# A two-layer hybrid backbone: 512-column projections, block transposes queued in the next block, other layouts and another order at the two ends

## The chip, the cores and the metric

The kernel runs on one core of a Trainium2 chip. The core has TensorE (PE: matrix products of 128x128 blocks of 32-bit numbers into PSUM, which has eight banks of 128x512), VectorE (DVE), ScalarE (ACT), GpSimd (POOL) and SyncE (SP), which here issues the loads from device memory. The metric is the device time of one launch in microseconds (us). Each kernel's runs are given by their median.

## The reference

```python
# layer 0: two recurrences as head groups, then a dense SwiGLU
u = modulate(rmsnorm(h), shift, scale)          # shift, scale: silu(cond) @ w_mod + b_mod
p = split(u @ w_in)                             # q, two gates, v, z of HGRN2; x, gate of RG-LRU
hg = gated linear attention over chunks of 64, both directions
rg = linear scan with gates of x, both directions
h = h + gate * (concat(rmsnorm(hg) * silu(z), rg * gelu(g)) @ w_out)
h = h + gate * ((silu(u2 @ w1) * (u2 @ w3)) @ w2)
# layer 1: neighbourhood attention, then top 2 of 8 experts
q, k, v = split(u @ w_qkv); q, k = rmsnorm per head
h = h + gate * (softmax(q k^T + bias, local window and all context keys) v @ w_o)
y = sum over the 2 best of 8 experts of weight_e * (silu(u2 @ w1[e]) * (u2 @ w3[e])) @ w2[e]
return h + gate * y                             # of the 256 latent tokens
```

There are 256 latent and 256 context tokens of width 1024; context tokens are modulated by a vector of their own. The hidden width is 2816, for the dense layer and for each expert. In the last layer only the latent tokens go through the experts.

## The kernel before

All weights are streamed from device memory once and the activations stay on the core. The loads go through one queue of SP, in program order, each into one of 15 slots of 1 MB; when no slot is free, the queue waits. Tokens are kept transposed (features on partitions, 512 tokens on columns).

A product of layer 0 and of the attention's projections is made in three matmuls (`mm3`, L157 to L160): each 32-bit operand is split into a high and a low part (`halves`, L131, on ACT and DVE: whi, wlo of the weights; Uhi, Ulo of the tokens), and high x high, high x low and low x high are summed. `proj_T` (L385) puts features on partitions, `proj_N` (L399) puts tokens there, in blocks of 256 columns: for each of two blocks and each tile of 128 tokens, 8 k-steps of three matmuls.

The beginning (L341 to L383): the two streams' tokens H0 are loaded, then blocks 2 and 0 of the modulation weights w_mod (scale and shift), the first chunks of w_in, and w_mod's blocks 3 and 1. `squares` (L306) and `rstd_rows` (L282) form the norm; `early_products` (L353) makes a row of modulation per block (L185), and `mod_finish` (L190) transposes it (L196). `modulate` (L321) writes Uhi and Ulo, first of k-steps 0 to 3, for which 48 matmuls follow, then of 4 to 7. In the recurrence that follows, steps of HGRN and matmuls of the projections share TensorE; the order is that of a scheduler with priorities, which writes it out ahead of time.

The experts (L1149 on): an expert has three blocks of hidden features (512, 512 and 384), a "unit" (e, j). `w13` makes silu(x w1) * (x w3) of up to 64 tokens of each of two tiles, on four 32-column strips of the array, and of a third group of 32 rows only if the expert has more than 64 tokens in a tile's share (`third_group`; experts 0, 1 and 3 take it here). `turn` (L1176) transposes a block's hidden rows hN into hT by matmuls with the identity, on 32-column strips; it is called in the next unit's w13 behind half of its k-steps. `down` (L1195) multiplies by w2, and `keep` (L1223) puts the expert's result into Y (three tiles of 128 rows hold four experts: 64 rows each in tiles 0 and 1, 32 each in tile 2). `gather` (L1097) collects the next experts' tokens with one-hot matrices (L1111, and L1064 for expert 0). After experts 3 and 7 `places` (L1239, one-hot matrices with the gates as values) and `scatter` (L1260) add Y back to the tokens; for experts 4 to 7 this stands around the last down() and at the end. `chores` is a list of such small works, of which one step is taken at each new weight chunk.

## Time and profile before

| | |
|---|---|
| runs (us) | 1697.43, 1701.37, 1702.54 |
| median | 1701.37 |
| profiled execution | 1702.45, its span 1700.7 |
| TensorE busy | 1598.6 of the span (94%) |
| VectorE, ScalarE, GpSimd busy | 721.1, 455.5, 56.0 |
| loads | 412.42 MB, mean 243 GB/s |

The profile is one execution. "Span" is the time from the first to the last instruction on record. Busy times of the engines overlap. A row such as `PE ... L1188 MATMUL ps_x<-ident,hN 128*32 128x128 f32 x64` is a run of 64 matmuls of line 1188 whose result lies in ps_x, made of ident and hN, on a 128x32 strip of the array; matmuls of 32-bit numbers on strips stand twice in the record. In brackets stands how long the engine was idle before, and what it waited for.

### The profile page before, as it was taken

The page shows a single profiled execution, that of the slowest core. Times are in us where ns is not written, and L with a number is a line of the kernel's source. Part 1 is how long each engine was busy: PE and PEld are TensorE (multiplying, and loading weights), DVE is VectorE, ACT ScalarE, POOL GpSimd, SP SyncE. Part 2 cuts the span into 40 slices and gives each one's busy share as a digit, 9 for nine tenths or more (in the row PEclk, how much of TensorE's full clock was granted, in tenths as well). Part 3 has the DMA queues.
Part 4 walks back from the last instruction along what each step waited for, and adds up shares of the span by engine and source line. Part 5 has one row for each costly group of instructions (what it writes and reads, how often), then busy time and mean ns, then how long its engine had stood idle before and what let it go on. Part 6 is the DMA issues. An engine that isn't in the chain of part 4 may idle for free. (4 is left out here: it accounts for less than half of the span.)

```text
span 1700.7 us, 29356 instructions
## 1 busy us (share of the span) xinstructions
PE 1598.6 (94%) x12668; PEld 1000.4 (59%) x12668; DVE 721.1 (42%) x1417; ACT 455.5 (27%) x795; POOL 56.0 (3%) x58
## 2 busy tenths in 40 slices
PE   6997989999999999999999999999999999998887
PEld 3675867788778788889984654343344334432222
DVE  6677456596874433678737520020202021201122
ACT  4574333433222222244536410010101010100000
POOL 0013141000000000000000000000000000000000
PEclk9999999999999999999998979999999999999999
DMA  9515123844475232534332298979999989999995
GB/s 342 170 63 173 50 75 124 295 140 149 149 246 174 87 99 99 173 115 159 125 124 76 103 364 302 352 275 398 414 415 413 416 352 411 414 414 412 410 400 229
DMA packets 153060, 412.42 MB, mean 243 GB/s; under 512 B 9552, under 2 KB 69328, under 8 KB 134864
## 3 DMA queue, kind: packets, MB, share of 16 engines
q1 hardware_dynamic: 152912, 410.28, 64.1%
q8 instruction: 113, 1.85, 0.5%
q14 instruction: 35, 0.29, 0.0%
HBM read 409.20 MB, written 1.05 MB: 241 GB/s over the span
## 5 line engine op out<-in xcount | busy, mean ns | idle before, releaser
L158 PE MATMUL ps_mm<-Uhi,whi 128*128 128x512 f32 (+1 forms) x576 | 223.5, 393 | 5.5 <-ACT Uhi L327 2.9
L1157 PE MATMUL ps_mm<-raw,X 128*32 128x512 f32 (+1 forms) x1920 | 212.1, 570 | 15.3 <-DMA raw<-in_moe_u 14.1
L160 PE MATMUL ps_mm<-Uhi,wlo 128*128 128x512 f32 (+1 forms) x576 | 222.4, 388 | 0.0
L159 PE MATMUL ps_mm<-Ulo,whi 128*128 128x512 f32 (+1 forms) x576 | 221.7, 388 | 0.0
L137 DVE TENSOR_TENSOR wlo<-raw,whi 128x1024 fp32r<-128x1024 f32 x134 | 164.9, 1239 | 114.7 <-ACT whi L137 109.9
L137 ACT CAST whi<-raw 128x1024 fp32r<-128x1024 f32 x134 | 139.1, 1049 | 274.0 <-PE ps_mm L159 208.9
L1157 PEld LDWEIGHTS ps_mm<-raw,X 128*32 128x32 f32 x1920 | 68.4, 111 | 140.8 <-issue 105.3
L1172 DVE TENSOR_TENSOR hN<-hs,ps_mm 128x512 f32<-128x512 f32 (+1 forms) x24 | 15.4, 643 | 300.4 <-PE ps_mm L1157 300.2
L158 PEld LDWEIGHTS ps_mm<-Uhi,whi 128*128 128x128 f32 x576 | 109.1, 191 | 31.6 <-ACT Uhi L327 3.3
L160 PEld LDWEIGHTS ps_mm<-Uhi,wlo 128*128 128x128 f32 x576 | 109.3, 190 | 23.6 <-issue 1.2
L159 PEld LDWEIGHTS ps_mm<-Ulo,whi 128*128 128x128 f32 x576 | 109.3, 190 | 23.5 <-issue 1.7
L1209 PE MATMUL ps_py<-raw,hT 128*32 128x512 f32 x928 | 113.4, 596 | 3.4 <-PEq L1142 1.7
L1170 ACT ACTIVATE hs<-ps_mm 128x512 f32<-128x512 f32 (+1 forms) x24 | 13.5, 561 | 374.2 <-PE ps_mm L1157 374.2
L408 PE MATMUL ps_mm<-whi,Uhi 128*128 128x256 f32 x384 | 110.9, 289 | 1.4 <-ACT Vn L547 1.0
L409 PE MATMUL ps_mm<-wlo,Uhi 128*128 128x256 f32 x384 | 109.7, 286 | 0.0
L410 PE MATMUL ps_mm<-whi,Ulo 128*128 128x256 f32 x384 | 109.6, 287 | 0.0
L236 DVE SCALAR_TENSOR_TENSOR macc<-raw,cond,macc 128x512 f32<-128x512 f32 x112 | 80.5, 748 | 6.4 <-DMA raw<-in_w_mod 5.7
L158 PE MATMUL ps_mm<-hh,whi 128*128 128x512 f32 (+1 forms) x224 | 77.9, 351 | 2.0 <-DVE H L688 1.6
L1157 PE MATMUL ps_mm<-wlo,X 128*32 128x512 f32 (+1 forms) x576 | 75.8, 555 | 3.8 <-DMA wlo<-in_moe_u 2.5
L160 PE MATMUL ps_mm<-hh,wlo 128*128 128x512 f32 (+1 forms) x224 | 77.7, 348 | 0.0
L159 PE MATMUL ps_mm<-hl,whi 128*128 128x512 f32 (+1 forms) x224 | 77.6, 347 | 0.0
L408 PEld LDWEIGHTS ps_mm<-whi,Uhi 128*128 128x128 f32 x384 | 72.8, 190 | 6.2 <-ACT Vn L547 2.4
(299 smaller groups left out, 2325.2 us busy)
## 6 DMA issues: line engine op xcount, KB each, us to landing
raw<-in_moe_u SPq DMA_DIRECT2D x83, 1024.0 KB, 13.1
raw<-in_moe_d SPq DMA_DIRECT2D x58, 1024.0 KB, 14.3
raw<-in_w_mod SPq DMA_DIRECT2D x48, 1024.0 KB, 5.4
raw<-in_ffn_w SPq DMA_DIRECT2D x33, 1024.0 KB, 5.3
raw<-in_moe_u SPq DMA_DIRECT2D x37, 768.0 KB, 10.8
wlo<-in_moe_u SPq DMA_DIRECT2D x45, 512.0 KB, 10.7
whi<-in_moe_u SPq DMA_DIRECT2D x45, 512.0 KB, 11.4
whi<-in_moe_d SPq DMA_DIRECT2D x30, 512.0 KB, 11.5
```

Source lines behind the costliest of these rows:

```text
L137: latest[:] = act.copy(hi, v), dve.tensor_tensor(lo, v, hi.bitcast(F32), op=OP.subtract)
L158: pe.matmul(o, sh, mh, start=start, stop=False)
L159: pe.matmul(o, sh, ml, start=False, stop=False)
L160: pe.matmul(o, sl, mh, start=False, stop=stop)
L236: dve.scalar_tensor_tensor(acc[s], w[:, j, :], c, acc[s], op0=OP.mult, op1=OP.add)
L408: pe.matmul(p, Uhi[:, k, tt], hi, start=k == 0, stop=False)
L409: pe.matmul(p, Uhi[:, k, tt], lo, start=False, stop=False)
L410: pe.matmul(p, Ulo[:, k, tt], hi, start=False, stop=k == KT - 1)
L1157: pe.matmul(p[b][32 * q:32 * q + 32, :], X[e][:, k, 32 * g:32 * g + 32], w[2 * b + a], start=k == 0, stop=k == KT - 1, tile_position=(0, 3 ...
L1170: act.activation(s[0][:, :fn], p[0], AF.Silu)
L1172: dve.tensor_tensor(h[0][:, :fn], s[0][:, :fn], p[1], op=OP.mult)
L1209: pe.matmul(PY[e][0][32 * q:32 * q + 32, :], hT_[:, c, CAP * a + 32 * g:CAP * a + 32 * g + 32], w[a][:, 512 * col:512 * col + 512], start= ...
```

## The change

Six edits.

1. The tokens (hT) and the modulation weights are laid out in device memory in the order in which they are read, so that each partition reads 8 KB in one piece (before: 1 KB of hT, 2 KB of w_mod).
2. Another order at the beginning: squares are made two k-slices at a time; the first chunk of w_in has 512 rows x 512 columns instead of 1024 x 256, and the second is loaded behind w_mod's blocks 3 and 1; the matmuls of three tiles for k-steps 0 to 3 come first, then the products of blocks 3 and 1, then the fourth tile's.
3. `proj_N` makes 512 columns at a time, with two chunks of 512 rows; all its tiles hold a PSUM bank until the second chunk. The norm of q and k (`qk_part`, `turn_qk`) follows in blocks of 512.
4. The first gather works on 32-column strips, and the second waits behind the first matmul of expert 0.
5. `turn` is made of 128x128 transposes, six for a full block, and is queued behind the fourth k-step of the next block. The third group's hidden rows lie in two halves on 128 partitions.
6. Y's rows are placed so that the last of four experts lies in tile 2 alone. Tiles 0 and 1 of experts 4 to 6 are scattered during expert 7, as chores; only tile 2 is left for the end. `keep` handles the third rows first.

```diff
+        if not kt:
+            v = raw.rearrange("p (k c) -> p k c", k=4)
+            sp.dma_start(v, src)
+            return v
...
-        return [stream(A["w_mod"][layer, 512 * half:512 * half + 512, 512 * blk:512 * blk + 512], 4, 512)
-                for half in range(2)]
-    def mod_products(p, ww):
-        for half, w in enumerate(ww):
+        return [stream(A["w_mod"][layer, blk, half]) for half in range(2)]
...
-    def squares(tp, h, s, acc):
+    def squares(tp, h, s, acc=None):
         c = slice(256 * s, 256 * s + 256)
-        for k in range(KT):
+        a = tp.tile([128, 2, NL], F32, name="sqa", tag="sqa", bufs=1)
+        for k in range(0, KT, 2):
             if k == 0:
-                act.activation(acc, h[:, k, c], AF.Square)
+                act.activation(a, h[:, k:k + 2, c], AF.Square)
             else:
-                sq = tp.tile([128, NL], F32, name="sq", tag="sq", bufs=2)
-                act.activation(sq, h[:, k, c], AF.Square)
-                dve.tensor_tensor(acc, acc, sq, op=OP.add)
+                sq = tp.tile([128, 2, NL], F32, name="sq", tag="sq", bufs=3)
+                act.activation(sq, h[:, k:k + 2, c], AF.Square)
+                dve.tensor_tensor(a, a, sq, op=OP.add)
+        acc = a[:, 0] if acc is None else acc
+        dve.tensor_tensor(acc, a[:, 0], a[:, 1], op=OP.add)
+        return acc
...
-            sp.dma_start(H0[:, :, NL * s:NL * s + NL], hT[:, :, NL * s:NL * s + NL])
+            sp.dma_start(H0[s], A["hT"][s])
...
+        def first_products(kk, tiles):
+            if not parts[kk]:
+                parts[kk] = [halves(wfirst[kk][:, 2 * i:2 * i + 2, :]) for i in range(2)]
+            for i in tiles:
+                for k in range(4):
+                    hi, lo = (x[:, k % 2, 128 * i:128 * i + 128] for x in parts[kk][k // 2])
+                    u = 4 * kk + k
+                    m = mm3(first[i], hi, lo, Uhi[:, u, :], Ulo[:, u, :], u == 0, u == KT - 1)
+            return m
...
-                wfirst = [stream(w_in[:, 2560 + 256 * m:2816 + 256 * m], KT, 256) for m in range(2)]
-            early_products(kk)
+                wfirst = [stream(w_in[0:512, 2560:3072], 4, 512)]
...
                 early.update((blk, mod_load(0, blk)) for blk in (3, 1))
-                first = [halves(v[:, :, 128 * i:128 * i + 128]) for v in wfirst for i in range(2)]
-                first = [(ps("mm"), hi, lo) for hi, lo in first]
-            for p, hi, lo in first if kk == 0 else ():
-                for k in range(4):
-                    mm3(p, hi[:, k, :], lo[:, k, :], Uhi[:, k, :], Ulo[:, k, :], k == 0, False)
+                wfirst.append(stream(w_in[512:1024, 2560:3072], 4, 512))
+                first = [ps("mm") for _ in range(4)]
+                m = first_products(0, range(3))
+                with behind(m):
+                    early_products(3)
+                with behind(m):
+                    m = early_products(1)
+                with behind(m):
+                    first_products(0, [3])
...
-    def proj_N(w, col, tiles, use, n=2):
-        for half in range(n):
-            w2 = weights(w[:, col + 256 * half:col + 256 * half + 256], KT, 256, "k")
+    def proj_N(w, col, tiles, use):
+        pp = {}
+        for kk in range(2):
+            w2 = weights(w[512 * kk:512 * kk + 512, col:col + 512], 4, 512, "k")
             for t in tiles:
-                p = ps("mm", 256)
+                p = pp[t] = ps("mm") if kk == 0 else pp[t]
                 tt = slice(128 * t, 128 * t + 128)
-                for k in range(KT):
-                    hi, lo = (x[:, k % 4, :] for x in w2[k // 4])
-                    pe.matmul(p, Uhi[:, k, tt], hi, start=k == 0, stop=False)
-                    pe.matmul(p, Uhi[:, k, tt], lo, start=False, stop=False)
-                    pe.matmul(p, Ulo[:, k, tt], hi, start=False, stop=k == KT - 1)
-                use(t, half, p)
+                for k in range(4):
+                    hi, lo = (x[:, k % 2, :] for x in w2[k // 2])
+                    u = 4 * kk + k
+                    pe.matmul(p, Uhi[:, u, tt], hi, start=u == 0, stop=False)
+                    pe.matmul(p, Uhi[:, u, tt], lo, start=False, stop=False)
+                    pe.matmul(p, Ulo[:, u, tt], hi, start=False, stop=u == KT - 1)
+                if kk:
+                    use(t, p)
             step()
...
-                pe.matmul(first[k // 4][:, CAP * (k % 4):CAP * (k % 4) + CAP], UN[:, t, 128 * k:128 * k + 128],
-                          DO[0][:, t, 0, :], start=t == 0 and k % 4 == 0, stop=t == 1 and k % 4 == 3)
+                for q in range(0, 128, 32):
+                    pe.matmul(first[k // 4][q:q + 32, CAP * (k % 4):CAP * (k % 4) + CAP],
+                              UN[:, t, 128 * k + q:128 * k + q + 32], DO[0][:, t, 0, :],
+                              start=t == 0 and k % 4 == 0, stop=t == 1 and k % 4 == 3, tile_position=(0, q))
...
+        after = opening if e2 == 0 else []
...
+                        with behind(*after):
...
-                at_half()
+                with behind(m):
+                    at_half()
...
-        dve.tensor_tensor(h[1][0:64, :fn], s[1][64:128, :fn], p[2][64:128, :], op=OP.mult)
+        for r, a, b in ((0, 0, 256), (64, 256, fn)):
+            dve.tensor_tensor(h[1][r:r + 64, 0:b - a], s[1][64:128, a:b], p[2][64:128, a:b], op=OP.mult)
...
-        for c0 in range(0, nc_, 2):
-            n = min(2, nc_ - c0)
-            p = ps("x", 2 * CAP * n)
-            for i, (r, w) in enumerate(((128, 64), (64, 32))):
-                for c in range(n):
-                    for q in range(0, 128, 32):
-                        f = 128 * (c0 + c) + q
-                        pe.matmul(sub(p[q:q + 32, :], 2 * CAP * c + 64 * i, [(CAP, 2), (1, w)]), h[i][0:r, f:f + 32],
-                                  ident[0:r, 0:r], start=True, stop=True, tile_position=(0, q), skip_group_check=True)
-            (act.copy if c0 else dve.tensor_copy)(hT_[:, c0:c0 + n, :].rearrange("p c t -> p (c t)"), p)
+        pp = [ps("x", 2 * CAP * n) for n in (2, nc_ - 2)]
+        for c, p in enumerate(pp):
+            for i in range(c, nc_, 2):
+                pe.transpose(sub(p, CAP * (i - c), [(CAP, 2), (1, 64)]), h[0][:, 128 * i:128 * i + 128], ident)
+        for c, p in enumerate(pp):
+            n = len(range(c, nc_, 2))
+            pe.transpose(sub(p, 64, [(2 * CAP, n), (CAP, 2), (1, 32)]), h[1][0:64 * n, 128 * c:128 * c + 128],
+                         ident[0:64 * n, 0:64 * n])
+        for c, p in enumerate(pp):
+            n = len(range(c, nc_, 2))
+            (act.copy if c else dve.tensor_copy)(sub(hT_[:, 0, :], 2 * CAP * c, [(4 * CAP, n), (1, 2 * CAP)]),
+                                                 p.rearrange("p (c t) -> p c t", c=n))
...
+        (k, at), (k3, at3) = PLACES[i]
+        for col in range(2):
             act.copy(t[64 * col:64 * col + 32, :], p[1][64 * col + 32:64 * col + 64, :])
         for col, c in enumerate(cols):
             r = slice(64 * col, 64 * col + 32)
             dve.tensor_tensor(t[r, :], t[r, :], p[1][r, :], op=OP.add)
-            dve.tensor_tensor(Y[32 * i:32 * i + 32, 2, c], t[r, :], gt2r[r, c], op=OP.mult)
+            dve.tensor_tensor(Y[at3:at3 + 32, k3, c], t[r, :], gt2r[r, c], op=OP.mult)
+        for col, c in enumerate(cols):
+            r = slice(64 * col, 64 * col + 64)
+            dve.tensor_tensor(Y[at:at + 64, k, c], p[0][r, :], gt2r[r, c], op=OP.mult)
...
+    PLACES = [((0, 0), (1, 64)), ((0, 64), (1, 96)), ((1, 0), (2, 96)), ((2, 0), (2, 64))]
+    DTS = {}
...
-    def half():
-        for DT in places(0):
+    def half(h, tiles):
+        for DTS[h] in places(h):
             yield
         for t, g in SETS:
             p = ps("x")
-            for i in range(3):
-                scatter(p, DT, t, g, [i])
+            for i in range(tiles):
+                scatter(p, DTS[h], t, g, i, i == 0, i == tiles - 1)
                 yield
             scattered(p, t, g)
...
-            for DT in places(1):
-                pass
-            acc = [ps("mm") if i < 3 else ps("x") for i in range(4)]
-            for p, (t, g) in zip(acc, SETS):
-                scatter(p, DT, t, g, [0])
         down(e, j)
         if (e, j) == (3, len(EBLOCKS) - 1):
-            chores.append(half())
-    for i in (1, 2):
-        for p, (t, g) in zip(acc, SETS):
-            scatter(p, DT, t, g, [i])
+            chores.append(half(0, 3))
+        if (e, j) == (6, len(EBLOCKS) - 1):
+            chores.append(half(1, 2))
+    while chores:
+        chore()
+    acc = [ps("mm") if i < 3 else ps("x") for i in range(4)]
+    for p, (t, g) in zip(acc, SETS):
+        scatter(p, DTS[1], t, g, 2, True, True)
...
-        "hT": np.concatenate([I["ctx"][0], I["x"][0]], axis=0).T,
-        "w_mod": I["w_mod"], "b_mod": I["b_mod"], "w_in": I["ev_w_in"][0], "w_out": I["ev_w_out"][0],
+        "hT": np.stack([I["ctx"][0], I["x"][0]]).reshape(2, NL, KT, 128).transpose(0, 3, 2, 1),
...
+        "w_mod": np.asarray(I["w_mod"]).reshape(2, 2, 4, 128, 12, 512).transpose(0, 4, 1, 3, 2, 5), "b_mod": I["b_mod"], "w_in": I["ev_w_in"][0], "w_out": I["ev_w_out"][0],
```

What the order shows on TensorE at three places follows (line, operation, result<-operands, shape, count). First the beginning: before, from the end of the first k-steps' matmuls (L158 to L160) over the products of the modulation (L185) and its transposes (L196) to the next matmuls.

```order
L160 MATMUL ps_mm<-Uhi,wlo 128x512
L158 MATMUL ps_mm<-Uhi,whi 128x512
L159 MATMUL ps_mm<-Ulo,whi 128x512
L160 MATMUL ps_mm<-Uhi,wlo 128x512
L185 MATMUL ps_md<-raw,cond 32x512 x16
L196 MATMUL ps_x<-ident,modrow 128x128 x8
L158 MATMUL ps_mm<-Uhi,whi 128x512 x3
```

Of the change, the same place; L162 to L164 are the three matmuls, L188 the products, L200 the transposes.

```order
L162 MATMUL ps_mm<-Uhi,whi 128x512
L163 MATMUL ps_mm<-Ulo,whi 128x512
L164 MATMUL ps_mm<-Uhi,wlo 128x512
L188 MATMUL ps_md<-raw,cond 32x512 x16
L200 MATMUL ps_x<-ident,modrow 128x128 x4
...
L200 MATMUL ps_x<-ident,modrow 128x128 x4
L162 MATMUL ps_mm<-Uhi,whi 128x512 x4
```

Twelve matmuls of the fourth tile now stand between the first four transposes and the second four (in place of the line of dots).

Second, a turn in expert 0, before: L1157 is w13, L1188 the turn, whose hN tiles are the first two and the third group of rows.

```order
L1209 MATMUL ps_py<-raw,hT 32x512 x32
L1157 MATMUL ps_mm<-raw,X_8035 32x384 x32
L1188 MATMUL ps_x<-ident,hN_8541 32x2x64 x8
L1188 MATMUL ps_x<-ident,hN_8542 32x2x32 x8
L1188 MATMUL ps_x<-ident,hN_8541 32x2x64 x8
L1188 MATMUL ps_x<-ident,hN_8542 32x2x32 x8
L1157 MATMUL ps_mm<-raw,X_8035 32x384 x5
```

Of the change, the same turn; L1193 is w13, L1225 and L1228 the turn.

```order
L1252 MATMUL ps_py<-raw,hT 32x512 x32
L1193 MATMUL ps_mm<-raw,X_7237 32x384 x32
L1225 MATMUL ps_x<-ident,hN_7766 128x2x64 x4
L1228 MATMUL ps_x<-ident,hN_7767 128x4x32 x2
L1193 MATMUL ps_mm<-raw,X_7237 32x384 x9
```

Thirty-two small matmuls became six full ones, at the same place here. One unit of expert 1 shows another place before, behind 8 of w13's matmuls and cut by 16 of down (L1209).

```order
L1157 MATMUL ps_mm<-raw,X 32x512 x8
L1188 MATMUL ps_x<-ident,hN_9007 32x2x64 x5
L1209 MATMUL ps_py<-raw,hT 32x512 x8
L1188 MATMUL ps_x<-ident,hN_9007 32x2x64 x3
L1188 MATMUL ps_x<-ident,hN_9008 32x2x32 x8
L1188 MATMUL ps_x<-ident,hN_9007 32x2x64 x8
L1188 MATMUL ps_x<-ident,hN_9008 32x2x32 x5
```

In the change a turn that has a next block stands behind 32 matmuls of its w13.

Third, the end, before: L1254 is the placing of experts 4 to 7, L1263 the scatter, L1209 and L1217 the last down(), rows of which are left out at the dots.

```order
L1254 MATMUL ps_x<-ident,D_14021 32x128 x11
L1263 MATMUL ps_mm<-Y,DT 32x512
L1209 MATMUL ps_py<-raw,hT 32x512 x8
L1263 MATMUL ps_mm<-Y,DT 32x512 x7
...
L1209 MATMUL ps_py<-raw,hT 32x512 x8
L1263 MATMUL ps_mm<-Y,DT 32x512 x12
L1263 MATMUL ps_x<-Y,DT 32x512 x4
L1263 MATMUL ps_mm<-Y,DT 32x512 x12
L1263 MATMUL ps_x<-Y,DT 32x512 x4
```

Of the change, the end from the last turn on; L1252 and L1260 are down, L1308 the scatter.

```order
L1228 MATMUL ps_x<-ident,hN_12731 128x4x32
L1252 MATMUL ps_py<-raw,hT 32x512 x24
...
L1252 MATMUL ps_py<-raw,hT 32x512 x24
...
L1252 MATMUL ps_py<-raw,hT 32x512 x8
L1308 MATMUL ps_mm<-Y,DT 32x512 x12
L1308 MATMUL ps_x<-Y,DT 32x512 x4
```

Nothing but down() stands behind the last turn until the 16 matmuls of the scatter.

## Rows read from the trace of the kernel before

**Rows 1.** The page: its first line, and the load rate in 40 slices.

```profile
span 1700.7 us, 29356 instructions
...
GB/s 342 170 63 173 50 75 124 295 140 149 149 246 174 87 99 99 173 115 159 125 124 76 103 364 302 352 275 398 414 415 413 416 352 411 414 414 412 410 400 229
```

**Rows 2.** Windows by stage: from:to, us, busy (count) of PE, PEld, DVE, ACT, POOL, granted clock, DMA share, GB/s.

```profile
0.00:41.00 41.00, 24.01 (x104) 15.31 (x104) 25.42 (x96) 17.69 (x35) 0.20 (x4) 0.96 0.99 342
110.00:290.00 180.00, 161.13 (x897) 123.53 (x901) 106.20 (x159) 69.16 (x101) 54.67 (x44) 0.97 0.29 99
994.00:1140.00 146.00, 145.12 (x1706) 62.49 (x1708) 16.11 (x29) 16.18 (x44) 0.00 (x0) 0.99 0.81 314
1140.00:1516.00 376.00, 362.04 (x4224) 143.00 (x4216) 55.70 (x100) 35.37 (x84) 0.00 (x0) 1.00 1.00 404
1516.00:1664.00 148.00, 123.21 (x1284) 35.30 (x1280) 23.48 (x46) 10.25 (x19) 0.00 (x0) 0.99 1.01 409
```

**Rows 3.** Timeline of the beginning: start, length, what, idle before it.

```profile
24.06 0.58 ACT L358 COPY modrow<-ps_md 128x512 f32<-128x512 f32 x1 [4.25 <-PE ps_md L185]
...
27.71 0.50 PE L158 MATMUL ps_mm<-Uhi,whi 128*128 128x512 f32 x1 [2.36 <-ACT whi L137]
...
48.92 1.62 PE L158 MATMUL ps_mm<-Uhi,whi 128*128 128x512 f32 x3 [1.70 <-ACT Uhi L327]
```

**Rows 4.** Windows of dense matmuls: of 512 columns, then of 256 (proj_N).

```profile
400.00:420.00 20.00, 20.00 (x88) 16.12 (x87) 7.84 (x9) 5.45 (x8) 0.00 (x0) 1.00 0.38 121
795.00:815.00 20.00, 20.00 (x172) 20.00 (x172) 11.48 (x34) 10.41 (x21) 0.00 (x0) 1.00 0.24 78
```

**Rows 5.** Timeline at the first gathers: strips (L1111), then the full array (L1064).

```profile
986.67 0.87 PE L1111 MATMUL ps_x<-DO,UN 128*32 128x192 f32 x8
...
990.91 3.73 PE L1064 MATMUL ps_py<-DO,UN 128*128 128x96 f32 x16
```

**Rows 6.** Timeline of turns and the w13 behind one.

```profile
1059.67 1.93 PE L1188 MATMUL ps_x<-ident,hN 128*32 128x128 f32 x64
1061.53 0.85 PE L1157 MATMUL ps_mm<-raw,X 128*32 128x384 f32 x8
...
1106.74 0.52 PE L1188 MATMUL ps_x<-ident,hN 128*32 128x128 f32 x9 [0.88 <-DVE hN L1172]
```

**Rows 7.** Timeline at a change from strips (L185) to the full array (L196).

```profile
43.70 1.92 PE L185 MATMUL ps_md<-raw,cond 128*32 128x512 f32 x16 [0.76 <-ACT modrow L358]
45.56 0.66 PE L196 MATMUL ps_x<-ident,modrow 128*128 128x128 f32 x4
```

**Rows 8.** Windows at the pause of the loads (columns as in rows 2).

```profile
1390.00:1395.00 5.00, 5.00 (x52) 1.53 (x48) 0.00 (x0) 0.00 (x0) 0.00 (x0) 1.00 0.59 245
1395.00:1400.00 5.00, 4.85 (x46) 1.39 (x42) 0.86 (x2) 1.08 (x2) 0.00 (x0) 1.00 0.29 76
```

**Rows 9.** Waits of PE from 990 to 1700 us: sum, count, longest.

```profile
PE ps_mm L1157 <- DMA raw<-in_moe_u: 14.1, 19, 2.0
PE ps_x L1188 <- DVE hN L1172: 12.9, 17, 1.0
```

**Rows 10.** The end: one window (columns as in rows 2), then the timeline.

```profile
1679.00:1682.00 3.00, 3.00 (x32) 1.10 (x28) 0.00 (x0) 0.00 (x0) 0.00 (x0) 1.00 0.16 66
...
1683.69 1.92 PE L1209 MATMUL ps_py<-raw,hT 128*32 128x512 f32 x16 [0.17 <-PEq L1142]
1684.87 1.39 DVE L1234 TENSOR_TENSOR y<-y,ps_py 32x512 f32<-32x512 f32 x2 [16.91 <-ACT y L1231]
...
1687.03 2.78 PE L1263 MATMUL ps_mm<-Y,DT 128*32 128x512 f32 x24 [1.42 <-DVE Y L1230]
1687.73 1.40 DVE L1235 TENSOR_TENSOR Y<-y,gt2r 32x512 f32<-32x512 f32 x2
...
1689.63 1.04 PE L1263 MATMUL ps_x<-Y,DT 128*32 128x512 f32 x8
...
1694.17 0.69 DVE L1268 TENSOR_TENSOR HN<-HN,ps_x 128x512 f32<-128x512 f32 x1 [0.17 <-PE ps_x L1263]
```

152 lines of the change are left out of this document (78 added, 74 removed).

## The prediction

> **What bounds the kernel now.** I read the page's GB/s line first, then the span cut into stages, then in each stage who is waited for. The GB/s line [rows 1] shows two kernels in one: up to about 990 us the loads run far under their best, and from there on nearly every slice stands near 400. The windows by stage [rows 2] say the same of TensorE. From 0 to 41 us it is busy for 24.01 of 41.00 us while the DMA engines are 0.99 busy at only 342 GB/s: the beginning waits for its loads and for the norm that follows them. From 110 to 290 us (the HGRN recurrence) it is busy for 161.13 of 180, so 18.9 us are idle between dependent steps. From 994 to 1140 us (experts 0 and 1, with the third 32-row groups) it is busy for 145.12 of 146 and the DMA share is 0.81: TensorE is the bound, and the load queue pauses because no buffer comes free. From 1140 to 1516 us the share is 1.00 at 404 GB/s: the loads are the bound. From 1516 to 1664 us TensorE is busy for 123.21 of 148 and waits for them. So an instruction saved is worth its time before 1140 us; behind it only what keeps the load queue from pausing counts, and then what stands behind the last load.
>
> The sum is made against the profiled execution, 1702.45 us, whose span is 1700.7 [rows 1]; the median of the runs is 1701.37, 1.1 lower.
>
> **1. Beginning.** The first projection matmul starts at 27.71 us, after the last evacuation of a modulation row at 24.06 [rows 3]. Ahead of these lie 2.1 MB of hT and 4.2 MB of w_mod. At 342 GB/s 6.3 MB take 18.4 us, at the 404 of the saturated stage [rows 2] 15.6. The new layout has the long pieces of the expert weights, which run at that rate, so at most 2.8 us; I take 1.8. The squares go from 16 to 8 ACT operations of twice the width; they follow the loads, so the row sums move with them. Then 36 instead of 48 matmuls (4 k-steps of three tiles) precede the products of blocks 3 and 1, and the fourth tile's 12 follow them and cover the modulation's transposes. TensorE resumed at 48.92 us after 1.70 idle [rows 3]. Blocks 3 and 1 now have 1 MB of w_in less ahead of them, 2.5 us at 404 GB/s. Together I take **-3** (-1 if the norm's chain on VectorE, into which two splits and the recurrence's masks are now sorted, holds the second half; -6 if both halves gain their load time).
>
> The Trainium skill ("DMA: Bandwidth & Descriptors", Specifications) puts line rate at pieces of 512 B and above, and the pieces of 1 and 2 KB here already are. By that page the new layout would give nothing, and the sum would be 1.8 us smaller; the 342 beside 404 GB/s at the same share of busy engines speaks against it.
>
> **2. Recurrence.** The same steps stand there, but the v projection between them now holds all four "mm" banks, and its 512-column matmuls are coarser filler. The order still puts more filler between the early steps than before. 18.9 us are idle [rows 2]; I take **-2** (-6 if a third of it goes, +4 if each of some 28 level steps waits 0.15 longer).
>
> **3. 512-column projections.** 1152 matmuls of 256 columns become 576 of 512. In a dense stretch of the first kind 172 take 20.00 us, 0.1163 each; of the second 88 take 20.00, 0.2273 [rows 4]. Two of the first cost 0.0053 more than one of the second: 576 x 0.0053 = 3.1 us at most. Some records can be missing from such a count, so **-2** (0 to -3.1). The weight loads are hidden in both (PEld 16.12 and 20.00 of 20).
>
> **4. Gather for expert 0.** 16 matmuls of 128x96 take 3.73 us [rows 5], 0.23 each. They become 64 on 32-column tiles. Eight such of 192 columns take 0.87 [rows 5], 0.11 each; at 96 columns I take half of that and less packing, 2.6 to 3.7 us for 64. About 10 matmuls of the next gather now queue behind the first expert matmul. **-0.7** (-1.5 to +0.5).
>
> **5. Experts 0 and 1, TensorE bound.** A block's turn is 64 records in 1.93 us [rows 6]. It becomes four plus two transposes of 128x128. Four such take 0.66 us [rows 7], so six 0.99; with 0.2 to return to the tiled form, 1.2. The turn now stands behind four k-steps of the next block instead of sometimes one, so its wait for hN (0.88 at 1106.74 [rows 6]) is covered: four k-steps are 32 records at 0.85 for 8 [rows 6], 3.4 us. Behind it, down() waits for hT; the other four k-steps lie between. Four turns in the stage: 4 x 0.73 + 0.88: **-3.8** (-2 to -9: other waits of this stage gone as well).
>
> **6. The pause at 1390 us.** The DMA share falls to 0.59 and 0.29 in two windows of 5 us [rows 8]: 0.41 x 5 + 0.71 x 5 = 5.6 us in which the queue stood full because TensorE had fallen behind. Between 1140 and 1390 about 8 turns gain 0.73 each, 5.8, and those of 17 waits for hN (12.9 us in all, mean 0.76 [rows 9]) that lie there another 5 or so. That is more than the pause, so it goes, with small ones beside it: **-6.2** (0 to -7). The waits for weights (14.1 us [rows 9]) then grow by what TensorE gains, and cost nothing more.
>
> **7. Tail.** The loads trail off at about 1679: the share is 0.16 from there to 1682 [rows 10]. The last down() matmuls end only at 1683.69 + 1.92 = 1685.6 [rows 10], since expert 7's placing (48 records) and a first part of its scatter (32 records, like those that take 3.64 us from 1687.03 to 1690.67 [rows 10]) stood in between. These move to units before, where TensorE waits for weights anyway; if that cover were gone the scatter's part alone would cost its 3.64 us again. Without them TensorE ends about 2 us behind the loads: -4.5. Behind that VectorE now forms the third rows first and then the 64 rows of both halves, both of which the one tile left to scatter needs. Against 1684.87, where it starts [rows 10], that is 1.39 + 1.40 + 0.70 = 3.5 us, 1688.4, for the first half; then 32 records, 3.64, and the last add, 0.69, with some 0.2 between: 1692.9 instead of 1694.17 + 0.69 = 1694.86 [rows 10]: -1.9. Together **-6.4** (-3 if the chore that scatters the other two tiles is not done by then; -8).
>
> Sum: -3 -2 -2 -0.7 -3.8 -6.2 -6.4 = -24.1; 1702.45 - 24.1 = 1678.4, and 1677 against the median.
>
> **Rivals.** *Switching the array.* If entering and leaving the full-array form each cost a whole tiled step of four records, 0.43 us [rows 6], a turn is 6 x 0.116 (a matmul of [rows 4]) + 0.86 + 0.1 = 1.7 and gains 0.25 instead of 0.73: terms 5 and 6 lose 4 x 0.48 = 1.9, and the hN waits alone still about cover the pause: 1679.5. For it: the entry at 45.56 us, where 4 transposes take 0.66 and not 4 x 0.116 = 0.46 [rows 7]. Chance 0.12. The Trainium skill ("TensorEngine Tiling (Array Packing)", Key Properties) says that changing the tiling mode drains the engine, which speaks against full transposes between tiled matmuls; 0.20 us of excess is all that this trace shows of it.
>
> *The weight stream hides it.* Terms 5 and 6 are given back: TensorE gains, but the buffers come free no earlier for the transfers that count, so 10 us don't come: 1687. For it, the share of 1.00 over 376 us [rows 2]; against it, the visible pauses. Chance 0.20.
>
> *The early pauses shrink too.* (1 - 0.81) x 146 = 27.7 us of pause lie in 994 to 1140 [rows 2]. If the earlier turns let half of these close beyond the 3.8 us that TensorE gains, 1664. Against it: TensorE is busy for 145.12 of 146 there. Chance 0.08.
>
> *The recurrence starves (other side).* The v projection takes all four "mm" banks for about 22 us (96 matmuls of 0.2273), and a dependent step whose own filler needs a bank waits for its evacuation. Each us of idle more in 110 to 290 is a us more in the end. From 38 us idle instead of 18.9 the gain is down to 3 (no change, chance 0.05); from 48 the kernel is slower, and at 50 to 55 it stands at 1708 (chance 0.05). For it: level steps already wait 18.9 us. Against it: the order shows more filler between the early steps, not less.
>
> **How the numbers follow.** The forecast has 0.50, the rivals 0.12, 0.20, 0.08, 0.05 and 0.05. The forecast's own bounds (sums of the terms' ends are unlikely together) give 1668 to 1684. The range for 8 in 10 takes in the stream rival with a little beyond and most of the early pauses: 1660 to 1691. A measurement tells 0.3%, 5 us, from no change; so faster means under 1696.3: 0.50 + 0.12 + 0.20 + 0.08 = 0.90, same 0.05, slower 0.05.
>
> **What would show it.** Of the changed kernel: first projection matmul near 26 us and the second half near 46; idle in the recurrence 15 to 18 us; a turn of 1.2 us (1.7: the first rival) without a wait on hN; a DMA share of 1.00 through 1370 to 1400 shifted by some 10 us (a pause still there: the stream rival); the end of TensorE's last down() 2.5 us after the last load, and one scatter of 32 records behind it. I am wrong if the recurrence's idle time grows by more than 10 us, or if the pause moves instead of going.

## The result

| | median (us) | range, runs | before beside it | ratio, 95% interval |
|---|---|---|---|---|
| the change | 1669.29 | 1667.77 to 1670.06, 4 | 1700.19 | 0.9818, 0.98 to 0.9835 |

The change is faster by 30.9 us, or 1.8%. The forecast was 1677, 24 us faster. The profiled execution took 1669.41 us, 33.0 less than that of before. All that follows compares these two executions stage by stage.

First the page of the change: its first line, and the load rate in 40 slices.

```profile
span 1667.6 us, 25716 instructions
...
GB/s 368 153 65 51 144 110 127 312 131 127 132 247 202 89 101 101 138 115 203 136 117 90 86 372 317 361 297 416 413 417 414 416 409 415 413 415 404 409 406 252
```

Next the windows by stage, with the columns of [rows 2]; the last three stages are taken 24 to 30 us earlier, about where the change reaches them.

```profile
0.00:41.00 41.00, 24.65 (x124) 14.25 (x124) 20.68 (x79) 14.64 (x26) 0.20 (x4) 0.96 0.96 368
110.00:290.00 180.00, 165.93 (x856) 122.11 (x855) 109.70 (x167) 72.93 (x104) 58.31 (x44) 0.98 0.30 105
970.00:1116.00 146.00, 145.38 (x1589) 62.37 (x1593) 19.61 (x53) 18.64 (x50) 0.00 (x0) 0.97 0.88 340
1110.00:1490.00 380.00, 360.93 (x3582) 134.12 (x3574) 59.60 (x120) 36.30 (x88) 0.00 (x0) 1.00 1.00 406
1490.00:1640.00 150.00, 128.84 (x1150) 37.95 (x1154) 29.71 (x63) 12.51 (x24) 0.00 (x0) 0.99 1.01 407
```

The load rate falls below 400 in two slices fewer between 990 us and the end (398 and 352 of [rows 1] are gone), and the idle time of the recurrence is 14.1 instead of 18.9 us (15.7 in 104 to 284 us, where the change has the recurrence some 6 us earlier). To see where the 33 us arose, the start of the same instruction is compared in both timelines. Of before: the last attention product of the recurrence (L619), the first matmul of the dense layer's second step, the first attention scores, the first of w_o, the first of the experts.

```profile
282.19 1.97 PE L619 MATMUL ps_hg<-At,Vn 128*128 128x256 f32 x8
...
415.92 0.40 PE L158 MATMUL ps_mm<-hh,whi 128*128 128x512 f32 x1
...
886.17 1.99 PE L858 MATMUL ps_mm<-kT,QT 64*128 64x512 f32 x8
...
951.72 0.50 PE L989 MATMUL ps_mm<-whi,Ahi 128*128 128x512 f32 x1
...
994.57 1.94 PE L1157 MATMUL ps_mm<-raw,X 128*32 128x512 f32 x8
```

Of the change the first projection, the second half behind it, the same five places, and then the end: the last down(), the scatter and the last add.

```profile
26.74 0.50 PE L162 MATMUL ps_mm<-Uhi,whi 128*128 128x512 f32 x1 [2.36 <-ACT whi L141]
...
47.55 1.52 PE L162 MATMUL ps_mm<-Uhi,whi 128*128 128x512 f32 x4 [2.28 <-ACT Uhi L337]
...
275.61 1.97 PE L650 MATMUL ps_hg<-At,Vn 128*128 128x256 f32 x8
...
414.60 0.39 PE L162 MATMUL ps_mm<-hh,whi 128*128 128x512 f32 x1
...
875.86 1.99 PE L889 MATMUL ps_mm<-kT,QT 64*128 64x512 f32 x8
...
937.68 0.50 PE L1020 MATMUL ps_mm<-whi,Ahi 128*128 128x512 f32 x1
...
977.03 1.97 PE L1193 MATMUL ps_mm<-raw,X 128*32 128x512 f32 x8
...
1651.31 1.92 PE L1252 MATMUL ps_py<-raw,hT 128*32 128x512 f32 x16 [0.46 <-DMA raw<-in_moe_d]
...
1655.79 4.48 PE L1308 MATMUL ps_mm<-Y,DT 128*32 128x512 f32 x24 [2.55 <-DVE Y L1280]
...
1661.19 0.69 DVE L1313 TENSOR_TENSOR HN<-HN,ps_x 128x512 f32<-128x512 f32 x1 [0.17 <-PE ps_x L1308]
```

The last steps of the way are read from the load windows: the end of the long pause of the loads behind expert 1, then the end of all loads. Of before, the end of the pause:

```profile
1138.00:1144.00 6.00, 5.13 (x59) 2.08 (x53) 1.38 (x2) 1.19 (x2) 0.00 (x0) 1.00 0.97 310
```

Of the change the end of the pause, the place of the second pause of before, the end of the loads and the scatter:

```profile
1114.00:1120.00 6.00, 6.00 (x63) 2.16 (x56) 0.68 (x1) 1.19 (x2) 0.00 (x0) 1.00 0.70 209
...
1370.00:1380.00 10.00, 9.85 (x90) 3.36 (x85) 0.69 (x1) 0.00 (x0) 0.00 (x0) 1.00 1.02 421
...
1649.00:1652.00 3.00, 2.54 (x24) 0.68 (x28) 0.00 (x0) 0.99 (x2) 0.00 (x0) 1.00 0.20 82
...
1655.00:1661.00 6.00, 5.21 (x32) 1.29 (x32) 3.44 (x6) 0.00 (x0) 0.00 (x0) 0.72 0.14 49
```

The pause ends near 1138 before and near 1116 in the change (0.70 x 6 us of its window are at work). The second pause of [rows 8] is gone. The loads run out 30 us earlier: their share is 0.20 from 1649 to 1652 us here and 0.16 from 1679 to 1682 before [rows 10], and it reaches zero near 1651 and 1681. So the lead grows like this:

| up to | lead (us) | gained in this stage | forecast |
|---|---|---|---|
| first projection | 1.0 | 1.0 | 3 for the whole beginning (term 1) |
| end of the recurrence | 6.6 | 5.6 | 2 (term 2) |
| second step of the dense layer | 1.3 | -5.3 | not in the forecast |
| first attention scores | 10.3 | 9.0 | 2 (term 3) |
| w_o | 14.0 | 3.7 | not in the forecast |
| first expert matmul | 17.5 | 3.5 | 0.7 (term 4) |
| end of the long pause | 22 | 4.5 | 3.8 (term 5) |
| end of the loads | 30 | 8 | 6.2 (term 6) |
| last add | 33.0 | 3 | 6.4 (term 7) |

The experts gave 15.5 of the 16.4 us forecast for them. What stands ahead of them gave 17.5 instead of 7.7. In the profile of e5 below, which is the change once more, the leads down to the first expert matmul are 0.8, 5.0, -1.4, 8.2, 14.8 and 17.1 us, so a single stage is known to some 3 us only.

### The profile page after: what moved, and what is told of

Same layout as the page of the kernel before. It is cut to its first block, busy times and chain, and to the rows that moved or that the text cites. A ratio compares the mean times of both kernels' runs of the same rounds, so it can differ in the third digit from the quotient of the medians.

```text
span 1667.6 us, 25716 instructions
## 1 busy us (share of the span) xinstructions
PE 1568.5 (94%) x10916; PEld 943.6 (57%) x10916; DVE 721.0 (43%) x1367; ACT 448.0 (27%) x735; POOL 60.4 (4%) x58
## 5 line engine op out<-in xcount | busy, mean ns | idle before, releaser
L1193 PE MATMUL ps_mm<-raw,X 128*32 128x512 f32 (+1 forms) x1920 | 217.2, 566 | 17.2 <-DMA raw<-in_moe_u 16.0
L162 PE MATMUL ps_mm<-Uhi,whi 128*128 128x512 f32 (+1 forms) x576 | 222.3, 392 | 5.8 <-ACT Uhi L337 3.4
L164 PE MATMUL ps_mm<-Uhi,wlo 128*128 128x512 f32 (+1 forms) x576 | 223.3, 389 | 0.0
L1193 PEld LDWEIGHTS ps_mm<-raw,X 128*32 128x32 f32 x1920 | 66.7, 110 | 142.6 <-issue 96.2
L162 PEld LDWEIGHTS ps_mm<-Uhi,whi 128*128 128x128 f32 x576 | 109.0, 191 | 32.1 <-ACT Uhi L337 3.9
L1232 DVE COPY hT<-ps_x 128x384 f32<-128x384 f32 x24 | 13.4, 558 | 259.6 <-PE ps_x L1228 259.6
L164 PEld LDWEIGHTS ps_mm<-Uhi,wlo 128*128 128x128 f32 x576 | 110.0, 191 | 23.7 <-issue 1.7
L1252 PE MATMUL ps_py<-raw,hT 128*32 128x512 f32 x928 | 110.5, 602 | 13.3 <-DMA raw<-in_moe_d 12.4
L1232 ACT COPY hT<-ps_x 128x384 f32<-128x384 f32 (+1 forms) x24 | 10.2, 425 | 317.5 <-PE ps_x L1228 317.5
L1252 PEld LDWEIGHTS ps_py<-raw,hT 128*32 128x32 f32 x928 | 31.1, 110 | 87.8 <-issue 66.9
L439 PE MATMUL ps_mm<-whi,Uhi 128*128 128x512 f32 x192 | 78.2, 407 | 0.0
L162 PE MATMUL ps_mm<-hh,whi 128*128 128x512 f32 (+1 forms) x224 | 77.7, 351 | 0.6 <-ACT hh L167 0.6
L1193 PE MATMUL ps_mm<-wlo,X 128*32 128x512 f32 (+1 forms) x576 | 75.0, 554 | 2.4 <-DMA wlo<-in_moe_u 1.2
L164 PE MATMUL ps_mm<-hh,wlo 128*128 128x512 f32 (+1 forms) x224 | 77.2, 346 | 0.0
L441 PE MATMUL ps_mm<-whi,Ulo 128*128 128x512 f32 x192 | 77.2, 403 | 0.0
## 6 DMA issues: line engine op xcount, KB each, us to landing
raw<-in_moe_u SPq DMA_DIRECT2D x83, 1024.0 KB, 14.1
raw<-in_moe_d SPq DMA_DIRECT2D x58, 1024.0 KB, 14.8
```

What stands on the lines that cost most here:

```text
L162: pe.matmul(o, sh, mh, start=start, stop=False)
L164: return pe.matmul(o, sl, mh, start=False, stop=stop)
L439: pe.matmul(p, Uhi[:, u, tt], hi, start=u == 0, stop=False)
L441: pe.matmul(p, Ulo[:, u, tt], hi, start=False, stop=u == KT - 1)
L1193: m = pe.matmul(p[b][32 * q:32 * q + 32, :], X[e][:, k, 32 * g:32 * g + 32], w[2 * b + a], start=k == 0, stop=k == KT - 1, tile_position=( ...
L1232: (act.copy if c else dve.tensor_copy)(sub(hT_[:, 0, :], 2 * CAP * c, [(4 * CAP, n), (1, 2 * CAP)]), p.rearrange("p (c t) -> p c t", c=n))
```

## The experiments

Each row gives the median of a kernel, its runs, and its ratio to the kernel before on the same chip. The change itself stands at 0.9817 or 0.9818; 0.001 is 1.7 us, and the intervals reach 0.0015 to 0.004 to each side. The change ran once more (e5) beside e6, e7 and e8; the others are compared with it by their ratios.

| run | median (us) | range, runs | ratio, 95% interval |
|---|---|---|---|
| e1, squares of the later norms as before | 1667.57 | 1663.93 to 1669.51, 4 | 0.9818, 0.9793 to 0.9842 |
| e2, projections of 256 columns | 1689.73 | 1686.58 to 1692.68, 6 | 0.9954, 0.9939 to 0.9969 |
| e3, turn in small matmuls | 1676.96 | 1676.27 to 1677.46, 4 | 0.9875, 0.9856 to 0.9895 |
| e4, end as before | 1673.29 | 1671.99 to 1675.19, 4 | 0.9859, 0.9839 to 0.9879 |
| e5, the change again | 1668.59 | 1666.43 to 1669.21, 4 | 0.9817, 0.9794 to 0.984 |
| e6, root first | 1666.78 | 1661.97 to 1670.38, 4 | 0.9818, 0.9793 to 0.9842 |
| e7, root first and 256 columns | 1682.88 | 1676.91 to 1686.45, 4 | 0.9903, 0.9866 to 0.9941 |
| e8, the experts' edits alone | 1683.93 | 1681.57 to 1687.96, 4 | 0.9919, 0.9893 to 0.9946 |
| e9, layout as before | 1667.37 | 1665.39 to 1672.71, 5 | 0.9805, 0.9787 to 0.9823 |
| e10, first gather as before | 1669.42 | 1667.8 to 1670.45, 5 | 0.9821, 0.9804 to 0.9839 |
| e11, turn not held back | 1672.0 | 1670.84 to 1676.18, 5 | 0.984, 0.982 to 0.986 |
| e12, root first, again | 1666.36 | 1663.84 to 1666.99, 5 | 0.9799, 0.978 to 0.9817 |

### The loss at the second norm

The timeline of the change shows what took 5.3 us back. These are VectorE's rows of the second stream's norm (rsq is the reciprocal root, macc the sums of the next layer's modulation), and TensorE's row that waits for it:

```profile
370.17 0.16 DVE L302 TENSOR_SCALAR rsq<-ps_hg 128x2 f32<-128x2 f32 x1 [0.41 <-PE ps_hg L289]
...
370.64 0.75 DVE L240 SCALAR_TENSOR_TENSOR macc<-raw,cond,macc 128x512 f32<-128x512 f32 x1
...
376.70 0.16 DVE L307 SCALAR_TENSOR_TENSOR rsq<-rsq,rsq 128x2 f32<-128x2 f32 x1
...
376.92 1.22 PE L295 MATMUL ps_hg<-ident,rsq 128*128 128x128 f32 x4 [3.92 <-DVE rsq L307]
```

The root takes from 370.17 to 376.86, 6.7 us, for eleven steps of 0.16, since a sum of 0.75 stands between many of them. TensorE waits 3.92 for its end, and then runs below its full clock, as the window around it shows:

```profile
366.00:390.00 24.00, 18.96 (x140) 18.46 (x140) 21.75 (x53) 8.99 (x19) 0.00 (x0) 0.86 0.13 44
```

The sums alone are not the cause. In the kernel before they stand between the same steps; its first and last step are:

```profile
372.86 0.15 DVE L296 TENSOR_SCALAR rsq<-ps_hg 128x2 f32<-128x2 f32 x1
...
379.82 0.16 DVE L301 SCALAR_TENSOR_TENSOR rsq<-rsq,rsq 128x2 f32<-128x2 f32 x1
```

That root takes 7.1 us, and TensorE does not wait for it: its matmuls last until 380.07, where the product with the root follows. But it starts 90.7 us behind the last attention product (282.19), and in the change 94.6 us behind it (275.61). What is new is that the root starts later.

e1 takes the squares back, with buffers of their own, for the later norms alone:

```diff
     def stream_rstd(tp, h, s):
-        return rstd_rows(squares(tp, h, s), V("invd"), 2)
+        acc = tp.tile([128, NL], F32, name="sqacc", tag="sqacc", bufs=2)
+        squares1(tp, h, s, acc)
+        return rstd_rows(acc, V("invd"), 2)
...
-            u = tp.tile([128, 2, NL], F32, name="u", tag="sq", bufs=3)[:, 0]
+            u = tp.tile([128, NL], F32, name="u", tag="u", bufs=4)
```

`squares1` is the squares of before.

> The change with only the squares of the two later norms (and their buffers) as before: 256 columns at a time, buffers of their own beside the modulation's. In the profile of the change TensorE waits 3.92 us for the second norm's reciprocal root at 377 us and then runs at half clock until some 383 us, and a lead of 7.8 us at the end of w_out is down to 1.5 us. Theory: the squares of the second stream come late because they go two k-slices at a time through three buffers that the modulation of the first stream also uses; with them as before the wait is gone and 4 to 6 us come back: 1663 to 1666. Rival: the sums of the next layer's modulation, sorted in between on VectorE, hold the chain whatever the squares are: 1668 to 1670.

The wait is gone from its profile, and the sums still stand between the steps; the first and the last:

```profile
367.69 0.15 DVE L302 TENSOR_SCALAR rsq<-ps_hg 128x2 f32<-128x2 f32 x1
...
374.65 0.15 DVE L307 SCALAR_TENSOR_TENSOR rsq<-rsq,rsq 128x2 f32<-128x2 f32 x1
```

The root again takes 7.1 us, but it starts 89.6 us behind the last attention product (278.06), and its product on TensorE follows the last matmul at 374.90 without a wait. From that attention product to the dense layer's second step it is 132.9 us, against 139.0 in the change and 133.7 before. On ScalarE the last squares end at 360.94, ahead of the Uhi of the first stream; in the change they end at 367.16, behind it. So the loss comes of the late squares, as the theory had it, and the rival fell. Still the whole is not told apart from the change (0.9818 both): of the 6.1 us 5.3 are given back by the first attention scores. A wait of 1.6 us stands at the end of the dense layer, as before, and one of 2.0 beside it.

e6 and e12 leave the squares and hold the sums back:

```diff
                     if half + j == 0:
-                        dve.tensor_scalar(acc[s], w[:, j, :], c, None, op0=OP.mult)
+                        with behind(*latest_y):
+                            dve.tensor_scalar(acc[s], w[:, j, :], c, None, op0=OP.mult)
```

> The change with one thing added: the sums of the next layer's modulation on VectorE may not be sorted in front of the last step of the norm's reciprocal root that was written last. Theory: these sums (0.7 us each, between small steps of the root) make the wait of 3.92 us at the second norm and the half clock behind it; without them 4 to 6 us go: 1661 to 1665. Rival: the root is late because its squares are, and the sums only fill the time; or what is gained there is given back at the next place that depends on VectorE: 1667 to 1670.

> The change with the sums held behind the root of the norm, again, in more rounds, since its first runs lie 1662 to 1670. Theory: 2 to 5 us faster than the change, 1663 to 1666. Rival: what is gained at the second norm is lost to half clock elsewhere, 1667 to 1669.

In e12 the root runs through, as VectorE's timeline shows:

```profile
368.87 0.16 DVE L303 TENSOR_SCALAR rsq<-ps_hg 128x2 f32<-128x2 f32 x1 [0.24 <-PE ps_hg L290]
...
371.04 0.16 DVE L308 SCALAR_TENSOR_TENSOR rsq<-rsq,rsq 128x2 f32<-128x2 f32 x1
371.12 0.48 DVE L239 TENSOR_SCALAR macc<-raw,cond 128x512 f32<-128x512 f32 x1
```

That is 2.3 us instead of 6.7, and the dense layer's second step begins there:

```profile
408.75 0.40 PE L162 MATMUL ps_mm<-hh,whi 128*128 128x512 f32 x1
```

It is 5.9 us earlier than in the change, of which 1.3 stand already where the root starts. So a short root ends the wait as well, with the late squares left as they are: it takes both, squares that come late and a root drawn out by the sums, and e1 and e12 each take one away. Of the 5.9, 3 arrive at the first expert, since the projections and the router behind it are some us longer there. Its first four runs, in e6, lie too far apart to tell, the five of e12 close together. The nine have a median of 1666.36 against 1669.1 for the eight of the change; their ranges overlap. By its median it is the fastest version that ran, about 2.7 us ahead of the change; by the ratios (0.9818 in e6, 0.9799 in e12) the lead lies between nothing and 3 us, so it is likely and not shown.

### The wide projections

e2 takes proj_N, qk_part and turn_qk from before; e7 does this with the addition of e6.

```diff
-    def proj_N(w, col, tiles, use):
+    def proj_N(w, col, tiles, use, n=2):
...
+        for half in range(n):
+            w2 = weights(w[:, col + 256 * half:col + 256 * half + 256], KT, 256, "k")
             for t in tiles:
+                p = ps("mm", 256)
```

> The change with the token projections in 256 columns again (with the norm of q and k in blocks of 256). Theory: the wider matmuls are worth the whole difference between two starts of 0.1236 us and one of 0.2357, 0.0114 x 576 = 6.6 us: 1675 to 1677. Rival, as forecast: 2 to 3 us for the matmuls, and the rest of what the projections gained is the wait on the norm ahead of them, which stays away: 1671 to 1673.

> The same addition, with the token projections in 256 columns again. The run with 256 columns was some 20 us slower than the change; its profile has 6.3 us of waits and 10.2 us of half clock at the attention's norm that the change does not have, and a later beginning of the recurrence. Theory: most of the 20 us is this wait, brought about by the order, and with the sums held back the wider matmuls are worth 6 to 9 us: 1670 to 1675. Rival: the 256 columns themselves cost it (matmuls and recurrence): 1682 to 1688.

Against the change e2 is slower by 0.0136 of the time of before, 23 us, more than both theories said. e7 lies where its rival put it, 0.0086 (14.6 us) behind the change and 0.0104 (17.7 us) behind e12. So the wide projections, with the order that they bring, carry about half of the whole gain or more. What it consists of is read between the dense layer's second step and the first scores. Before:

```profile
415.92:886.17 470.25, 465.59 (x2642) 396.69 (x2640) 278.31 (x525) 152.44 (x239) 0.00 (x0) 1.00 0.42 140
```

The change:

```profile
414.60:875.86 461.26, 460.68 (x2162) 371.73 (x2160) 269.62 (x451) 147.53 (x199) 0.10 (x1) 1.00 0.42 143
```

TensorE's busy time falls by 4.9 us, and 4.1 us of idle time go. 960 matmuls of 256 columns became 480 here. From start to start one of 256 takes 0.118 us (18 of them from 883.83 to 885.96 before) and one of 512 takes 0.232 (nine of them from 868.70 to 870.79 in e12), so a pair costs some 0.005 more than a single one, 2 to 3 us in all; where the other 2 to 3 us of busy time went is open. In e2 stands this wait:

```profile
PE ps_x L250 <- DVE macc L240: 4.5, 1, 4.5
```

Here TensorE waits 4.5 us for the same sums on VectorE, queued ahead of the norm. With the sums held behind the root (e7) some 8 of e2's 23 us go; about 15 stay. The theory that most of it was this wait fell. What stays lies partly in the recurrence: in e7 it ends 4.3 us later than in e12, and the scores begin 15.3 later. From the first projection matmul to the last attention product e7 takes 254.1 us, as before (254.5), and e12 249.1, as the change (248.9).

### The turn, its place and the end

e3 puts the small matmuls back behind the same fourth k-step, with the layout of the third group's rows that belongs to them; e11 keeps the transposes and takes the hold away.

```diff
             if k == KT // 2 - 1 and at_half:
-                with behind(m):
-                    at_half()
+                at_half()
```

> The change with the turn in small matmuls on 32-column strips again, still queued behind the fourth k-step. Theory of the forecast: TensorE sets the pace in experts 0 and 1, four turns of some 0.9 us more delay the loads by 3 to 4 us there, and some 8 turns later give back part of the margin that keeps the queue from pausing near 1390 us, 0 to 5.6 us more: 1673 to 1679. Rival, the weight stream hides the turn: 1669 to 1671.

> The change with the turn's transposes no longer held behind the fourth k-step: the order puts most of them at the end of the block, right ahead of or between the first matmuls of down() that need them. Theory: the place is half of the turn's gain, since there each turn waits for the copies into hT and nothing covers them, 0.5 to 1 us in each of 24: 1671 to 1678. Rival: only the form counts, since in most units TensorE waits for weights anyway: 1667 to 1670.

e3 is 0.0057 slower, 9.7 us, at the upper end of its theory; e11 0.0022, 3.7 us, within its theory, but at the edge of the intervals. In e3 the long pause ends some 6 us later, of which 2.5 stand already at the first expert matmul, and a trace of the second is back:

```profile
1114.00:1120.00 6.00, 6.00 (x82) 3.10 (x78) 0.00 (x0) 1.03 (x4) 0.00 (x0) 1.00 0.01 3
...
1370.00:1380.00 10.00, 9.85 (x90) 3.09 (x82) 2.07 (x3) 1.19 (x2) 0.00 (x0) 1.00 0.94 374
```

In e11 the waits for hN are back, 16 of them, and with them a pause at 1370:

```profile
1370.00:1380.00 10.00, 9.85 (x90) 3.34 (x86) 2.91 (x5) 1.19 (x2) 0.00 (x0) 1.00 0.76 290
...
PE ps_x L1224 <- DVE hN L1210: 13.4, 16, 1.1
```

So the form of the turn counts, and by these waits its place too, with less. The rival by which the weight stream hides the turn fell in e3. The turn itself, in the change's timeline:

```profile
1015.63 0.66 PE L1225 MATMUL ps_x<-ident,hN 128*128 128x128 f32 x4
1016.12 0.38 PE L1228 MATMUL ps_x<-ident,hN 128*128 128x128 f32 x2
1016.43 0.86 PE L1146 MATMUL ps_x<-DO,UN 128*32 128x192 f32 x16
```

From its first transpose to the next matmul on strips are 0.80 us, against 1061.53 - 1059.67 = 1.86 in [rows 6].

e4 takes Y's rows, the placing and the scatter of before.

```diff
-        if (e, j) == (6, len(EBLOCKS) - 1):
-            chores.append(half(1, 2))
...
+    for i in (1, 2):
+        for p, (t, g) in zip(acc, SETS):
+            scatter(p, DT, t, g, [i])
```

> The change with the end as before: Y's rows as before, the placing and the first part of the scatter of experts 4 to 7 around the last down(), two parts of the scatter behind it. Theory: the end behind the last load is 5 to 6 us longer: 1674 to 1676. Rival: the last down() waits for its loads anyway and the placing fits into these waits, so only the second half of the scatter counts, 2 us: 1671 to 1672.

It is 0.0041 slower, 7.0 us by the ratios and 4.7 by the medians against e5, between its rival and its theory, nearer to the theory. e8 is the kernel before with the change's turn, its place, Y's rows and the end:

> The kernel before with the change's turn, its place, its halves of the third group, Y's rows and the end, and nothing else of it. Theory, by the forecast's terms 5 to 7: 3.8 + 6.2 + 6.4 = 16 us faster than before: 1681 to 1685. Rival, the weight stream hides all but the end: 5 to 7 us faster, 1691 to 1694.

It is 14.65 us faster than before by the medians, 13.8 by the ratio, within the theory and outside the rival.

### Layout and first gather

e9 loads the tokens and w_mod as before, and e10 gathers for expert 0 as before.

```diff
-            sp.dma_start(H0[s], A["hT"][s])
+            sp.dma_start(H0[s], A["hT"].rearrange("(k p) t -> p k t", p=128)[:, :, NL * s:NL * s + NL])
...
-        after = opening if e2 == 0 else []
+        after = []
```

> The change with the tokens and the modulation weights laid out in device memory as before (pieces of 1 and 2 KB for each partition). Theory of the forecast: the first 6.3 MB come at some 342 GB/s instead of 368 to 404, and the first projection matmul and all behind it stand 1 to 2 us later: 1669 to 1671, with 340 to 350 GB/s in the first 41 us. Rival, pieces of that size already run at the full rate: 1667 to 1669 and the same GB/s as the change.

> The change with the first gather on the full array and the second not held back, as before. Theory, by the rows (64 matmuls on strips in 2.79 us, 16 full ones in 3.73): 1 us slower at the beginning of the experts, 1669 to 1671. Rival: the 3.5 us that the stretch from the router to the first expert matmul became shorter are all this edit's, 1671 to 1673.

e9 is no slower (0.9805). Its first projection starts at 26.53 us, that of the change at 26.74, although the loads ran at 350 instead of 368 GB/s over the first 41 us. So the theory of the forecast fell: the layout gives nothing that can be measured. e10 is not told apart from the change (0.9821), and within its theory's bounds.

## Why the forecast was right, and where it was short

The direction was right, and so was the sum for the experts, by most of its steps. Ahead of them the forecast was 9.8 us short between the profiled executions. That the whole came within 7 us is partly luck: terms that were too small (2, 3 and 6) stand beside terms that were too large (1 and 7) and a loss that was not foreseen. A slip in the last rival bore on nothing: with 50 to 55 us idle its own sum gives 1710 to 1715, not 1708.

**Term 1, the beginning (3 us, measured 1.0 at the first matmul, 1.4 at the second half).** The step "342 against 404 GB/s" failed. e9 has the old layout and loses nothing. The Trainium skill ("DMA: Bandwidth & Descriptors", Specifications) has pieces of 512 B and above at the full rate; by that rule the gain is nil, and e9 agrees, with a first matmul at 26.53 against 26.74. The mean rate over 41 us says nothing of the loads that are waited for: in e9 it is 350 GB/s, and the start is the same. The bound for VectorE's chain, -1, was the true one: TensorE waits 2.28 us for Uhi at 47.55, and ScalarE's Uhi waits for a step of VectorE at 46.40, behind two splits of weights from 43.90 to 46.25. Whether the remaining 1.0 comes of the squares or of the chunk is open; it wasn't tried, and between executions of the same beginning the first matmul moved as much (25.43 us in e4, 26.95 in e5).

**Term 2, the recurrence (2, measured 5.6).** The mechanism, more filler between the early steps, fits: in the change the waits for Qt (L576 before, L607 and L642 now) are shorter, 7.4 us instead of 10.7. Before and then the change:

```profile
PE ps_hg L576 <- DVE Qt L590: 10.7, 9, 2.4
```

```profile
PE ps_hg L607 <- DVE Qt L621: 4.0, 6, 1.3
PE ps_hg L642 <- DVE Qt L621: 3.4, 1, 3.4
```

Other waits grew (for kd from 1.6 to 3.8 us), and e7 shows that the gain came with the wide projections; that the filler is the reason was not tested alone. The bound of -6 held it. The rival of starving banks fell.

**Term 3, the projections (2, measured 9.0 for the stage).** The price of a pair was right: some 0.005 by the starts above, 0.0053 in the forecast. What the term put at nothing without a reason are the waits of this stage: 4.1 us of idle time went, 2.7 at the attention's norm and 1.6 at the end of the dense layer among them. The 1.6 are hardly a gain of the projections: in e1, which has the projections of the change and reaches that place 3.6 us earlier, they are back. Of the 4.9 us of busy time 2 to 3 are not accounted for.

**What was not in the forecast.** The squares of edit 2 were counted for the beginning alone; at the second norm they come late, and 5.3 us were lost, as e1 shows. And TensorE's clock: behind the first scores TensorE waited 1.6 us in the kernel before and twice 0.6 in the change, and the granted clock behind it stood lower for longer. The windows from the scores on, before:

```profile
880.00:900.00 20.00, 18.26 (x86) 11.23 (x84) 10.52 (x26) 9.42 (x21) 0.24 (x1) 0.80 0.33 125
900.00:952.00 52.00, 49.15 (x287) 26.02 (x287) 39.21 (x109) 34.68 (x86) 0.00 (x0) 0.94 0.16 46
```

The same of the change, and its first window in e5, the same kernel:

```profile
869.00:889.00 20.00, 18.80 (x70) 10.55 (x70) 10.96 (x27) 9.58 (x19) 0.24 (x1) 0.83 0.38 137
889.00:938.00 49.00, 47.18 (x281) 25.02 (x282) 38.92 (x107) 35.35 (x86) 0.00 (x0) 1.00 0.17 49
...
869.00:889.00 20.00, 18.80 (x86) 11.90 (x86) 11.49 (x29) 10.85 (x22) 0.24 (x1) 1.00 0.43 140
```

The levels are 2.4 and 1.2 GHz, so a mean of 0.80 over 20 us is 8 us at the lower one and costs up to 4. In these windows that makes 0.20 x 20 + 0.06 x 52 = 7.1 us lost before, and 0.17 x 20 = 3.4 in the change, as much as the 3.7 of this stage. But e5, with the same two waits of 0.6, keeps the full clock, and so does e2 with the wait of 1.6: the stage takes 65.6 us before, 61.8 in the change, 59.0 in e5 and 59.2 in e2. So the fall comes in some executions and not in others, and the 3.7 cannot be put down to the change. At the router the same working gives 0.28 x 30 = 8.4 us before (granted clock 0.72 from 975 to 1005) against 0.19 x 27 = 5.1 (0.81 from 961 to 988): 3.3 of the 3.5 there, in one execution of each. So term 4 (0.7) may be right in size; e10 shows 0.5 us for it, which is not told apart from nothing.

**Terms 5 and 6 (10.0, measured 12).** The turn takes 0.80 us where 1.2 was forecast, and the waits for hN are gone but for one. The pause at 1390 went by the step that the forecast gave. The rival of early pauses did not come: up to the end of the long pause the stage gave 4.5 us where 3.8 were forecast. The rival of the drained array fell in its size: the Trainium skill ("TensorEngine Tiling (Array Packing)", Key Properties) says that a change of tiling mode drains the engine, and here something of it can be seen. Eight transposes between matmuls on the full array take 0.88 us from start to start (285.11 to 285.99 in the change), 0.11 each, so six would take 0.66 of the 0.80 us; and the first of the turn follows the eight matmuls ahead of it by 1.01 us (1014.62 to 1015.63), where the next eight follow by 0.86 (1013.76 to 1014.62). Both changes together cost some 0.3 us a turn, by this estimate, where the rival had 0.86.

**Term 7, the end (6.4, measured 3; 4 in e5).** The first part was mis-sized by a reading: the loads trail off at 1679, but they end near 1681, where the next 1 us window has none. So the last down() stood 1685.61 - 1681 = 4.6 us behind them, not 6.6, and now 1653.23 - 1651 = 2.2: that gave 2.4 instead of 4.5. The second part gave 0.6 instead of 1.9: from the last down() to the end of the last add are 1661.88 - 1653.23 = 8.65 us against 1694.86 - 1685.61 = 9.25 [rows 10]. TensorE now waits 2.55 us for Y, and its clock is 0.72 in the window of the scatter, so that 24 records take 4.48 us and not 2.78 [rows 10]. In e5 the same wait is followed by the full clock:

```profile
1657.21 2.78 PE L1308 MATMUL ps_mm<-Y,DT 128*32 128x512 f32 x24 [2.55 <-DVE Y L1280]
```

There the end behind the last down() takes 6.95 us, 2.3 less than before, so the step itself was right.

## What to carry to other kernels

Add up the waits of a stage beside the price of its instructions; here the waits that went (4.1 us) were worth more than the price of the wide matmuls (2 to 3 us). When an edit makes the input of a short dependent chain on VectorE later, look up how long TensorE's own work covers that chain: the sums between the steps of the root cost nothing until the squares came 4 us later. Before a difference between two profiles is put down to an edit, compare two profiles of one kernel. A stage bound by loads still gains from faster compute, as long as the load queue pauses somewhere for want of a buffer.
